# A hybrid decoder block in float32: operand addresses, eight projection pieces ahead of attention, and stores moved back

## The chip, the cores and the metric

The kernel runs on one core of a Trainium2 chip. It is judged by the device time of one launch in microseconds, over three runs; lower is better. TensorE (PE) multiplies, VectorE (DVE), ScalarE (ACT) and GpSimd (POOL) work element by element, and SyncE (SP) issues the transfers between the memories, one after the other in its queue.

## The reference, cut to what matters

One layer for one sequence of 2048 tokens of width 1024. Half of the input projection feeds eight heads of stick-breaking attention, the other half four groups of causal pooling over 2, 4, 8 and 16 tokens; both go through one output projection, and a SwiGLU FFN of width 2816 follows. Norms are modulated by a vector that is itself a product of c with w_cond.

```python
h = rmsnorm(x, g_mix_pre[l]) * (1.0 + scale_m) + shift_m
q, k, v, u = jnp.split(h @ w_in[l], [512, 1024, 1536], axis=-1)
attn = stick_breaking_attention(to_heads(q), to_heads(k), to_heads(v))
pool = pooling_mixer(u, w_pool[l], pool_scale[l])
mix = jnp.concatenate([attn, pool], axis=-1) @ w_out[l]
x = x + gate_m * rmsnorm(mix, g_mix_post[l])
h = rmsnorm(x, g_ffn_pre[l]) * (1.0 + scale_f) + shift_f
f = (jax.nn.silu(h @ w_gate[l]) * (h @ w_up[l])) @ w_down[l]
x = x + gate_f * rmsnorm(f, g_ffn_post[l])
```

Attention weighs a key by sigmoid(z) times the product of sigmoid(-z) over all later keys up to the query, with z = q.k / 8.

## The kernel before, in words

**Numbers.** A product of two float32 matrices is three matmuls of split operands: each operand is cut into a high part (a ScalarE copy to fp32r, L59) and the rest (a subtraction on VectorE or GpSimd, L60), and mm3 (L65) issues high x high, high x rest and rest x high. Each is 128x128 against 128x512.

**Order.** Inside manual_schedule (L140) TensorE, ScalarE, VectorE and GpSimd issue their instructions in the order in which the program writes them. SP is left out of that: a scheduler places its transfers, by readiness in its own model and, among those that are ready, by the place in the program. Once placed, SP takes them strictly one after the other: a store whose data isn't there holds every load behind it.

**Stages.** (1) Projections of token blocks 0 and 1 (a block is 512 tokens, a task is one 128-column chunk of q, k or u for one block). pieces (L434) yields after each of the eight mm3 of a task; run_small (L408) then does one small thing: an urgent one (taking a finished product out of its bank) or the next step of a pooling group. Beside it, rest_of_cond (L285) streams w_cond through four wc buffers and the four quarters of spare; VectorE sums it up (acc, L210). Weight chunks are loaded into w32 (two buffers, L424) 20 pieces ahead and split 14 to 5 pieces ahead (LOAD_AT, SPLIT_AT, L40). (2) v for all tokens (v_pieces, L480), with the tokens of blocks 2 and 3 prepared beside it. (3) Attention, 80 units of four steps (L984): z (L828), two sigmoids, a running product on VectorE (scan, L844 and L847), the product w on GpSimd (L852), four transposes (L863), a split, and the product with v (L878). Between its steps, fillers (L898) put the pieces that project q, k and u of blocks 2 and 3: N_PIECES = 217, spread in proportion to the area of the steps (goal, L1002). (4) The output projection. (5) The FFN in two halves of the tokens, gate and up then down, each a product of 2x2 blocks done with seven products instead of eight; a step of it is twelve matmuls. Its split weights come from operand (L1041): five of six from ring, every sixth from fx.

**What the change touches.** store_qk (L353) takes a finished q or k product, splits it into a buffer e (two of them for blocks 0 and 1) and stores it. pool_ops (L360) takes u, makes running sums on us0 and us1, then the mean um (L395, L399), and stores it (L400); um has one buffer, as up has bufs=1. take_chunk (L471) queues both. attending (L406) says that attention has begun.

**Places in memory.** Pools are stacked: const, c1, wst, up, att, qk from the left (later const, then ring and the FFN's token operands), and wsp, ha, hb, hc, tok, cond or wv from the right (later fx). Each tile's size is rounded up to 32 bytes for each partition. Before, const ends 288 bytes past a multiple of 512, so that ring and the FFN's operands behind it start there; up ends 192 past one, with vt and sg behind it; the six pr tiles of 513 words (2080 bytes each) lie between sg and w, so that w starts at 384, wth and wtl at 64, kt and qt at 128. On the right, all large tiles start at 480, but for xt in tok and the pools behind it (wvh and wvl among them), which start at 224.

Of the kernel before, what the change touches and what calls it, by code (L numbers as in the profile page):

```python
# [9 lines left out]
F32 = mybir.dt.float32  # L10
# [7 lines left out]
P = 128  # L18
# [10 lines left out]
TB = 512  # L29
# [4 lines left out]
OFF = 7  # L34
PRB = 6
# [9 lines left out]
def block_kernel(ctx, tc, x, c, w_cond, b_cond, g_mix_pre, g_mix_post, w_in, w_pool,  # L45
                 pool_scale, w_out, g_ffn_pre, g_ffn_post, w_gate, w_up, w_down, out):
    nc = tc.nc
# [6 lines left out]
    def raw(ap):  # L54
        return ap.bitcast(F32)

    def split(hi, lo, src, low=nc.vector):

        nc.scalar.copy(hi, src)  # L59
        low.tensor_tensor(lo, src, raw(hi), ALU.subtract)  # L60
# [12 lines left out]
    def open_pool(stack, name, bufs=1, side=None):  # L73
        kw = {"side": side} if side else {}
        return stack.enter_context(tc.tile_pool(name=name, bufs=bufs, reuse_waits="tile", **kw))

    dram = ctx.enter_context(tc.tile_pool(name="dram", bufs=1, space=DRAM))
    const = ctx.enter_context(tc.tile_pool(name="const", bufs=1))

    def dt(name, shape):  # L80
        return dram.tile(shape, F32, tag=name, name=name)
# [4 lines left out]
    mtd = [dt(f"mtd{i}", [KC, P, TB]) for i in range(NTB)]  # L86
# [16 lines left out]
    mods = {n: const.tile([P, KC], F32, tag=n, name=n) for n in ("af", "bf")}  # L103
    mods["am"], mods["bm"] = sumsq[:, 0:KC], sumsq[:, KC:]

    fx = None

    def ft(tag, name, shape=(P, TB)):
# [33 lines left out]
    c1 = open_pool(ph1, "c1")  # L142
# [26 lines left out]
        nc.gpsimd.memset(rcnt[:, j:j + 1], 1.0 / (j + 1))  # L169
    colv = c1.tile([P, 68], F32, tag="colv", name="colv")  # L170
    cs = c1.tile([P, KC], F32, tag="cs", name="cs")
    halo = [c1.tile([P, 16], F32, tag=f"halo{g}", name=f"halo{g}") for g in range(NG)]

    hts = ExitStack()
# [3 lines left out]
    pro = ExitStack()  # L178
    hc = open_pool(pro, "hc", side="right")
    tokp = open_pool(pro, "tok", bufs=2, side="right")  # L180
    condst = ExitStack()
    cond = open_pool(condst, "cond", bufs=2, side="right")
    ht = {}
# [169 lines left out]
    def store_qk(tb, ps, dst, name):  # L353
        pool, tag, bufs = (tokp, "e", 2) if tb < 2 else (wst, "e", 1)
        both = pool.tile([P, 2, TB], F32R, tag=tag, bufs=bufs, name=f"{name}_{tb}")
        split(both[:, 0], both[:, 1], ps)
        nc.sync.dma_start(dst[tb].rearrange("l p t -> p l t"), raw(both))
        stored.add((name[0], int(name[1]), tb))

    def pool_ops(tb, ps, g):  # L360

        win = 2 << g
        u = up.tile([P, 16 + TB], F32, tag="u", name=f"u{g}_{tb}")

        m = None
        if tb > 1:
            m = up.tile([P, TB], F32, tag="um", name=f"um{g}_{tb}")

        def take():
            if m is None:  # L370
                nc.scalar.copy(u[:, 16:], ps)
            else:
                nc.scalar.mul(u[:, 16:], ps, 1.0 / win)
                nc.scalar.copy(m, ps)
            if tb == 2:
                nc.scalar.mul(u[:, 0:16], halo[g], 1.0 / win)
            else:
                nc.gpsimd.tensor_copy(u[:, 0:16], halo[g])
            nc.gpsimd.tensor_copy(halo[g], u[:, TB:TB + 16])
        yield take  # L380
        prev, step, ahead, n = u, 1, 1, 0
        while step < win:
            cur = up.tile([P, 16 + TB], F32, tag=f"us{n % 2}", name=f"us{g}_{tb}_{step}")
            yield lambda: (nc.gpsimd if attending else nc.vector).tensor_tensor(cur[:, ahead:], prev[:, ahead:],
                                                  prev[:, ahead - step:16 + TB - step], ALU.add)
            prev, step, ahead, n = cur, 2 * step, ahead + 2 * step, n + 1
        if m is None:
            m = up.tile([P, TB], F32, tag="um", name=f"um{g}_{tb}")

        def mean():  # L390
            if tb > 1:
                nc.gpsimd.tensor_tensor(m, prev[:, 16:], m, ALU.subtract)
                nc.sync.dma_start(mtd[tb][4 + g], m)
                return
            nc.vector.scalar_tensor_tensor(m, prev[:, 16:], 1.0 / win, u[:, 16:], ALU.mult, ALU.subtract)  # L395
            if tb == 0:
                first = up.tile([P, 16], F32, tag="uf", name=f"uf{g}")
                nc.vector.tensor_tensor(first[:, 0:win], prev[:, 16:16 + win], rcnt[:, 0:win], ALU.mult)
                nc.vector.tensor_tensor(m[:, 0:win], first[:, 0:win], u[:, 16:16 + win], ALU.subtract)  # L399
            nc.sync.dma_start(mtd[tb][4 + g], m)  # L400
        yield mean


    small, urgent = [], []
    stored = set()
    attending = False  # L406

    def run_small():  # L408
        if urgent:
            urgent.pop(0)()  # L410
        elif small:
            op = next(small[0], None)
            if op is None:
                small.pop(0)
                run_small()
            else:
                op()
# [80 lines left out]
    def drain_small():  # L498
        while small or urgent:
            run_small()  # L500

    def weave(main, sides):

        done = [0] * len(sides)
        for n, _ in enumerate(main):
            for i, (ops, first, every) in enumerate(sides):
                if n >= first + done[i] * every:
                    done[i] += 1
                    next(ops, None)
        for ops, _, _ in sides:  # L510
            for _ in ops:
                pass
# [281 lines left out]


    att = open_pool(ph1, "att", bufs=2)
    qkp = open_pool(ph1, "qk", bufs=2)
    kv = {}

# [87 lines left out]
    def unit_loads(u):  # L887
        h, tb, sc = u
        if sc == tb:
            assert tb < 2 or {("q", h // 2, tb), ("k", h // 2, tb)} <= stored  # L890
            qts[h, tb] = block_loads(h, tb)
# [6 lines left out]
    def fillers():  # L898
        yield from pieces(1, chunks, tasks, [first_filler])
        while urgent:  # L900
            urgent.pop(0)()
# [3 lines left out]
    fill = fillers()  # L905
    N_PIECES = 9 * 2 * len(chunks) + 1
    units = [(h, tb, sc) for half in range(2) for h in range(HEADS) for tb in (2 * half, 2 * half + 1) for sc in range(tb, -1, -1)]
    area = [2.5 if tb == sc else 4.0 for _, tb, sc in units]
    wo, wo_next = [], 0
    HB_FREE = N_PIECES - 18  # L910
    END = 79
    POOL_EVERY = 2
    taken = 0
    attending = True
    begin = psum("z2", 1, "begin")
    nc.vector.memset(begin, 0.0)
# [4 lines left out]
    def wo_load():  # L921
        nonlocal wo_next
        for l in range(2):
            nc.sync.dma_start(raw(wo[wo_next][l]), wod[wo_next][l])
        wo_next += 1
# [24 lines left out]
    def mix_split(T, m32):  # L950
        mh = wsp.tile([P, KC, P], F32R, tag="wh", name=f"mh_{T}")
        ml = wsp.tile([P, KC, P], F32R, tag="wl", name=f"ml_{T}")
        for half in range(2):
            ks = slice(4 * half, 4 * half + 4)
            split(mh[:, ks], ml[:, ks], m32[:, ks])
        return T, mh, ml
# [26 lines left out]
    spent = 0.0  # L983
    for n in range(len(steps) + OFF):  # L984

        late_values = len(waiting) > LAG and waiting[0][0][1] == waiting[0][0][2] and waiting[0][1] == 0
        if len(waiting) > LAG and not late_values:
            values_step(*waiting.pop(0))
        if n < len(steps):
            u, i = steps[n]  # L990
            if i == 0:
                unit_loads(u)
            weights_step(u, i)
            spent += 2.5 if u[1] == u[2] else 4.0
        if len(scans) > 1 or n >= len(steps) and scans:
            scan_step(*scans.pop(0))
        if n >= OFF:
            u, b = steps[n - OFF]
            waiting.append((u, b, *turn_step(u, b)))
        if late_values:  # L1000
            values_step(*waiting.pop(0))
        goal = N_PIECES * spent / (4 * sum(area[:END]))  # L1002
        while fill is not None and taken < goal:
            taken += 1
            if next(fill, 0) == 0:
                fill = None

        if small and (n > len(steps) if fill is None and len(small) == 1 else n % POOL_EVERY == 0):
            run_small()
        for pool, here in ((hb, not wo and taken >= HB_FREE), (ha, len(wo) == 4 and fill is None)):  # L1010
            if here:
                hi, lo = (pool.tile([P, 4, D], F32R, tag=tag, name=f"wo_{pool.name}{tag}")
                          for tag in ("hi", "lo"))
                wo.extend((hi[:, k, :], lo[:, k, :]) for k in range(4))
        if wo_next < len(wo):
            wo_load()
        if n in FIRST_LOADS:
            firsts.append(mix_load(SEQUENCE[FIRST_LOADS.index(n)]))
        if n in FIRST_SPLITS:
            products.append(mix_products(*mix_split(*firsts.pop(0))))  # L1020
        if n in FIRST_ADDS:
            firsts[0] = mix_add(*firsts[0])
        if n >= len(steps):
            mix_pieces(PER_STEP)
# [690 lines left out]
```

## Time and profile before

| | us |
|---|---|
| median of 3 runs | 2284.33 (2283.15 to 2285.94) |
| the profiled execution | 2285.23 |
| its span | 2283.4 |

Stages in that execution: the projections to about 180 us, v to 286, attention from 292 to about 812, the output projection to about 1010, the FFN from there on. The page gives the engines' busy time, the clock that TensorE was granted, and the chain of work that ended last, followed back from the end. A row of the timeline holds start, duration, engine, line and operation, with its output and inputs, and in brackets the idle time ahead of it and who ended it. A matmul's duration includes its way through the array, so that one starts before the last has ended: the pace is the distance between starts. A row of the windows holds the stretch, its length, the busy time and count of TensorE, weight loads, VectorE, ScalarE and GpSimd, then the granted clock, the share of the DMA engines and GB/s. A row of the waits holds who waited for whom, the sum, the count and the longest.

### The profile page before, as it was taken

How to read it: one execution, taken by the hardware profiler on the slowest of the kernel's cores; microseconds unless marked ns; L12 is line 12 of the kernel's file. 1: busy time of each engine (PE TensorE's matmuls, PEld its weight loads, DVE VectorE, ACT ScalarE, POOL GpSimd, SP SyncE). 2: the span in 40 equal slices, each digit the busy share in tenths (PEclk: the TensorE clock that was granted, in tenths of full speed). 3: DMA queues.
4: the chain of work that ended last, by engine and by line, in shares of the span. 5: the costliest groups of instructions: out<-in, count | busy, mean ns of one | idle time of the engine just before them, and what ended most of it. 6: DMA issues, size and time to landing. Idle time of an engine off the chain costs nothing.

```text
span 2283.4 us, 33237 instructions
## 1 busy us (share of the span) xinstructions
PE 2247.0 (98%) x10605; PEld 1847.4 (81%) x10605; DVE 1619.5 (71%) x2212; ACT 1166.1 (51%) x2418; POOL 1295.7 (57%) x1607
## 2 busy tenths in 40 slices
PE   7999989999999999999999999999999999999998
PEld 5778878888888878887888888888888888888887
DVE  6774589999999966667656566786766565655566
ACT  4334579998899854443232323554533333334444
POOL 3552267787779965546777777331476565651003
PEclk9999999999999999999999999999999999999999
DMA  8885776634444356665545455776753332328654
GB/s 295 306 272 199 282 203 186 172 111 112 116 131 109 123 192 217 218 226 164 164 157 161 159 159 187 264 248 208 259 175 123 94 116 93 115 89 291 214 186 147
DMA packets 323979, 413.55 MB, mean 181 GB/s; under 512 B 20630, under 2 KB 189146, under 8 KB 323676
## 3 DMA queue, kind: packets, MB, share of 16 engines
q1 hardware_dynamic: 319484, 409.07, 55.7%
q10 hardware_dynamic: 4320, 2.36, 0.4%
q8 instruction: 83, 1.36, 0.2%
q14 instruction: 92, 0.75, 0.1%
HBM read 282.90 MB, written 128.45 MB: 180 GB/s over the span
## 4 chain that ended last, share of the span: by engine, by line
PE 90%; DVE 3%; ACT 2%; DMA 2%; POOL 2%; issue 1%; SPq 0%; DVEq 0%; POOLq 0%; ACTq 0%
PE wt L863 5%; PE t_g L69 3%; PE t_g L70 3%; PE t_u L70 3%; PE t_u L69 3%; PE t_u L71 3%; PE t_g L71 3%; PE dn0p L70 3%; PE dn0p L71 3%; PE dn0p L69 3%; PE dn1p L70 3%; PE dn1p L69 3%; PE dn1p L71 3%; PE b_u L70 3%; PE b_g L70 3%; PE b_g L69 3%
## 5 line engine op out<-in xcount | busy, mean ns | idle before, releaser
L852 POOL TENSOR_TENSOR w<-sg,pr 128x512 f32<-128x512 f32 (+2 forms) x320 | 306.7, 958 | 53.3 <-DVE pr L847 18.8
L1230 POOL TENSOR_TENSOR s<-s,cu 128x512 f32<-128x512 f32 x88 | 132.3, 1510 | 239.4 <-DVE cu L1229 146.5
L847 DVE TENSOR_TENSOR_SCAN pr<-pr,carry,begin 128x512 f32<-128x512 f32 x192 | 243.8, 1270 | 0.0
L831 ACT ACTIVATE sg<-z 128x512 f32<-128x512 f32 (+2 forms) x320 | 181.5, 567 | 54.4 <-PE z L829 44.3
L60 DVE TENSOR_TENSOR wtl<-wt,wth 128x512 fp32r<-128x512 f32 (+1 forms) x320 | 189.2, 591 | 19.9 <-ACT wth L59 18.2
L59 ACT CAST wth<-wt 128x512 fp32r<-128x512 f32 (+1 forms) x320 | 181.0, 567 | 11.9 <-PE wt L863 11.9
L833 ACT ACTIVATE pr<-z 128x512 f32<-128x512 f32 (+2 forms) x320 | 180.9, 565 | 0.0
L863 PE MATMUL wt<-ident,w 128*128 128x128 f32 x1088 | 172.2, 273 | 0.7 <-POOL pr L843 0.4
L60 DVE TENSOR_TENSOR u_s_l<-u_s,u_s_h 128x512 fp32r<-128x512 f32 x66 | 65.3, 989 | 145.9 <-ACT u_s_h L59 140.7
L863 PEld LDWEIGHTS wt<-ident,w 128*128 128x128 f32 x1088 | 134.0, 140 | 30.7 <-POOL pr L843 0.9
L1220 ACT ACTIVATE s<-s 128x512 f32<-128x512 f32 x88 | 55.7, 633 | 182.7 <-DVE s L1219 182.7
L878 PE MATMUL av<-wth,vt 128*128 128x512 f32 (+1 forms) x320 | 126.2, 394 | 1.7 <-ACT o L883 1.4
L828 PE MATMUL z<-kt,qt 128*128 128x512 f32 (+2 forms) x320 | 118.5, 370 | 6.6 <-DMA kt<-kd 5.1
L60 DVE TENSOR_TENSOR u_a_l<-u,u_a_h 128x512 fp32r<-128x512 f32 x66 | 73.0, 1108 | 71.0 <-ACT u_a_h L59 71.0
L70 PE MATMUL dn0p<-w0p_l,g0p_h 128*128 128x512 f32 x308 | 120.8, 392 | 0.6 <-DVE w0p_l L60 0.6
L69 PE MATMUL dn0p<-w0p_h,g0p_h 128*128 128x512 f32 x308 | 120.5, 391 | 0.0
L71 PE MATMUL dn0p<-w0p_h,g0p_l 128*128 128x512 f32 x308 | 120.3, 391 | 0.0
L879 PE MATMUL av<-wtl,vt 128*128 128x512 f32 (+1 forms) x320 | 117.6, 368 | 1.7 <-DVE wtl L60 1.4
L829 PE MATMUL z<-kt,qt 128*128 128x512 f32 (+2 forms) x320 | 117.1, 366 | 0.0
L844 DVE TENSOR_TENSOR_SCAN pr<-pr,zero,begin 128x128 f32<-128x128 f32 (+3 forms) x128 | 111.2, 870 | 7.0 <-ACT pr L833 6.6
L70 PE MATMUL dn1p<-w1p_l,g1p_h 128*128 128x512 f32 x292 | 114.4, 392 | 0.0
L69 PE MATMUL dn1p<-w1p_h,g1p_h 128*128 128x512 f32 x292 | 114.2, 391 | 0.0
(692 smaller groups left out, 7063.8 us busy)
## 6 DMA issues: line engine op xcount, KB each, us to landing
g<-in_w_gate_dram SPq DMA_DIRECT2D x42, 512.0 KB, 5.3
u<-in_w_up_dram SPq DMA_DIRECT2D x42, 512.0 KB, 4.1
wc<-in_w_cond_dram SPq DMA_DIRECT2D x32, 512.0 KB, 7.1
qt<-qd SPq DMA_DIRECT2D x64, 256.0 KB, 3.9
kt<-kd SPq DMA_DIRECT2D x96, 128.0 KB, 3.3
vt<-vd SPq DMA_DIRECT2D x48, 256.0 KB, 3.8
wd<-in_w_down_dram SPq DMA_DIRECT2D x44, 256.0 KB, 3.5
tdt<-wd SPq DMA_DIRECT2D x44, 256.0 KB, 2.0
```

The lines of the kernel that those rows point to most:

```text
L59: nc.scalar.copy(hi, src)
L60: low.tensor_tensor(lo, src, raw(hi), ALU.subtract)
L69: nc.tensor.matmul(ps, lh, rh, start=first and i == 0, stop=False)
L70: nc.tensor.matmul(ps, lh, rl, start=False, stop=False)
L71: nc.tensor.matmul(ps, ll, rh, start=False, stop=last and i == n - 1)
L831: nc.scalar.activation(sg[:, 0:L], z[:, 0:L], AF.Sigmoid, scale=0.125)
L833: nc.scalar.activation(pr[:, 0:L], z[:, 0:L], AF.Sigmoid, scale=-0.125)
L847: nc.vector.tensor_tensor_scan(keys, keys, begin, carry, ALU.mult, ALU.bypass)
L852: nc.gpsimd.tensor_tensor(w[:, 0:L], sg[:, 0:L], pr[:, 1:L + 1], ALU.mult)
L863: nc.tensor.transpose(wt[:, i * P:(i + 1) * P], wss[u][i][:, b * P:(b + 1) * P], ident)
L878: nc.tensor.matmul(av[:, lo0:], vb, wh[:, lo0:], start=first, stop=False)
L1230: nc.gpsimd.tensor_tensor(s, s, u, ALU.mult)
```

## The change

Three things. **Addresses:** lay_out allocates tiles that nothing uses. A pad of 192 bytes ends const, one of 96 bytes lies in c1, one of 64 bytes ends att, and one of 256 bytes lies in tok behind its small tiles, which now come first; in att the order is now vt, sg, w, wth, wtl, and pr and the carries behind them. With that, the large tiles of const's neighbours start 480 bytes past a multiple of 512 on both sides: ring and the FFN's operands, vt, sg, w, wth, wtl, kt, qt, wvh and wvl. The identity stays at 128, and the pr tiles keep their odd size. **Eight pieces:** the first eight pieces of the fillers (one task: q of head pair 0, block 2) are issued ahead of attention; the rest are spread over it as before. **Stores:** the store of a q or k product is issued four run_small later, that of a mean ten run_small later; run_stores counts them down, and drain_small or the start of attention issues what is left. In attention stores go at once, as before.

```diff
+    def lay_out(pool, tags, pad):
+        for tag, bufs, words in tags:
+            pool.tile([P, words], F32, tag=tag, bufs=bufs, name=f"first_{tag}")
+        pool.tile([P, pad], F32, tag="pad", bufs=1, name="pad")
+
+    lay_out(const, (), 48)
...
+    lay_out(c1, (), 24)
...
+    lay_out(tokp, (("ss", 2, 1), ("rs_v", 2, 1), ("rs_r", 4, 1)), 64)
...
-        nc.sync.dma_start(dst[tb].rearrange("l p t -> p l t"), raw(both))
+        later(4, lambda: nc.sync.dma_start(dst[tb].rearrange("l p t -> p l t"), raw(both)))
...
-            nc.sync.dma_start(mtd[tb][4 + g], m)
+            later(10, lambda: nc.sync.dma_start(mtd[tb][4 + g], m))
...
-    small, urgent = [], []
+    small, urgent, waiting_stores = [], [], []
+
+    def later(pieces, store):
+        if attending:
+            store()
+        else:
+            waiting_stores.append([pieces, store])
+
+    def run_stores(pieces):
+        for entry in list(waiting_stores):
+            entry[0] -= pieces
+            if entry[0] <= 0:
+                waiting_stores.remove(entry)
+                entry[1]()
...
     def run_small():
+        run_stores(1)
...
     def drain_small():
         while small or urgent:
             run_small()
+        run_stores(100)
...
+    lay_out(att, (("vt", 6, TB), ("sg", 5, TB), ("w", OFF + 4, TB), ("wth", 4, TB), ("wtl", 4, TB), ("pr", PRB, TB + 1),
+                  *((f"carry{i}", 2, 1) for i in range(4))), 16)
...
+    START = 8
     POOL_EVERY = 2
-    taken = 0
+    for _ in range(START):
+        next(fill)
+    taken = START
+    run_stores(100)
     attending = True
...
-        goal = N_PIECES * spent / (4 * sum(area[:END]))
+        goal = START + (N_PIECES - START) * spent / (4 * sum(area[:END]))
```

## The prediction

> **What bounds the kernel now.** I read the page first (busy shares, chain of waits), then TensorE's own waits, then the windows by stage.
>
> ```profile
> PE 2247.0 (98%) x10605; PEld 1847.4 (81%) x10605; DVE 1619.5 (71%) x2212; ACT 1166.1 (51%) x2418; POOL 1295.7 (57%) x1607
> ...
> PE 90%; DVE 3%; ACT 2%; DMA 2%; POOL 2%; issue 1%; SPq 0%; DVEq 0%; POOLq 0%; ACTq 0%
> ```
> ```profile
> PE z L828 <- DMA kt<-kd: 5.1, 1, 5.1
> PE u L71 <- POOL wu_l L60: 3.0, 1, 3.0
> ```
> TensorE works 98% of the span and 90% of the chain that ended last, so time comes only from two places: the few stalls of TensorE, and the pace of its matmuls. The two waits shown are the ones that this change can reach: the first z of attention waits for keys, and one projection waits for a split weight. Whether attention itself is TensorE's is less clear:
>
> ```profile
> 400.00:500.00 100.00, 100.00 (x579) 85.16 (x578) 97.79 (x132) 91.95 (x216) 80.06 (x177) 1.00 0.51 146
> 600.00:700.00 100.00, 100.00 (x565) 84.33 (x565) 98.39 (x123) 90.97 (x199) 77.82 (x171) 1.00 0.39 113
> ```
> Columns: TensorE, weight load, VectorE (97.8 and 98.4 of 100 us), ScalarE, GpSimd, clock, DMA. VectorE is 2% from being the bound there.
>
> **Part 1, addresses.** In the program of before, the pools on the left from ring on begin 288 bytes past a multiple of 512, and fx on the right 480 past one. const holds 672 bytes (the 128x128 identity 512, mhalf 32, sumsq 64, af and bf 32 each) from 128 on: 800 = 512 + 288. The new pad of 48 words (192 bytes) makes it 480, as on the right. In the FFN operand() takes every sixth operand from fx, so the two operands of a product differ by 0, 192 or 320 bytes modulo 512. Here are the first matmuls of six successive steps of 12:
>
> ```profile
> 1053.17 0.39 PE L69 MATMUL t_g<-t2h,g_s_h 128*128 128x512 f32 x1
> ...
> 1055.89 0.39 PE L69 MATMUL t_g<-t3h,g_s_h 128*128 128x512 f32 x1
> ...
> 1058.63 0.39 PE L69 MATMUL t_g<-t1h,g_s_h 128*128 128x512 f32 x1
> ...
> 1061.35 0.39 PE L69 MATMUL t_g<-t4h,g_a_h 128*128 128x512 f32 x1
> ...
> 1064.07 0.39 PE L69 MATMUL b_g<-b22h,g_s_h 128*128 128x512 f32 x1
> ...
> 1066.87 0.39 PE L69 MATMUL b_u<-b11h,u_a_h 128*128 128x512 f32 x1
> ```
> Twelve matmuls take 2.72 us where both operands lie in pools at 288 (t2, t1, t4), 2.74 with a weight from fx against tokens at 288 (t3, difference 192), and 2.80 with b22 on the right at 480 against a weight at 288 (difference 320). The size follows from the counts. Down: 2 x 7 phases x 11 chunks less the 4 held ones are 150 chunks, in each third the w operand lies in fx: 50 chunks at +0.08 us. Gate and up: 22 b22 steps in the first half, less those with a weight from fx, are 19 more at +0.08; about 48 steps at +0.025. Sum 69 x 0.08 + 48 x 0.025 = 5.5 + 1.2 = **6.7 us**, all on TensorE's path. I take -6.5 (bounds 0 and -7.5). In attention kt and qt already agree (both at 128), wth against vt differs by 128 and will agree; the trace has no case of it alone, so I count 0 (at most 1 us: 0.002 us for each of about 600 matmuls, the 192 case as the nearest). The pads themselves hold no instruction.
>
> The Trainium skill speaks against this part: SBUF — State Buffer, "Who interferes with whom", says that TensorE has two independent read ports and never waits on anyone. By that rule the part is worth 0. The rows above disagree with it by 0.08 us in 2.72, but they don't isolate the address from the pool it belongs to, so the rule's outcome is a rival below.
>
> **Part 2, stores later.** The chain of waits through the projections:
>
> ```profile
> 100.57 9.07 DMA wq<-in_w_in_dram
> ...
> 113.86 1.11 DVE um L395
> 115.27 0.33 SPq L400
> 115.65 0.42 SPq L202
> 116.12 5.94 DMA wu<-in_w_in_dram
> ...
> 125.46 2.55 POOL spare L264
> 128.00 1.68 POOL wu_l L60
> ```
> ```profile
> 108.62 1.22 DVE L275 TENSOR_TENSOR acc<-acc,spare 128x1024 f32<-128x1024 f32 x1
> ```
> ```profile
> 97.00 4.68 POOL L60 TENSOR_TENSOR wu_l<-wu,wu_h 128x256 fp32r<-128x256 f32 x4 [4.95 <-ACT wu_h L59]
> ```
> ```profile
> 129.73 0.50 PE L71 MATMUL u<-hth,wu_l 128*128 128x512 f32 x1 [2.96 <-POOL wu_l L60]
> ```
> SP stands before the store of um (L400) until VectorE has finished um, at 115.27; behind it are a load into spare (L202) and the load of wu, which ends in TensorE's wait of 2.96 us. The spare half is free at 109.84 (108.62 + 1.22), the earlier wu buffer at 101.7 (97.00 + 4.68). With the store ten pieces (10 x 3 x 0.227 = 6.8 us) further back, wu can be issued near 110.3 rather than 116.1. The DMA engines set a limit:
>
> ```profile
> 110.00:120.00 10.00, 9.74 (x50) 7.97 (x51) 8.06 (x10) 2.11 (x6) 6.55 (x8) 1.00 0.90 318
> 120.00:130.00 10.00, 7.04 (x31) 5.51 (x31) 6.49 (x8) 4.38 (x8) 6.04 (x5) 1.00 0.96 344
> ```
> They are 90 to 96% busy, so about 1.4 us of transfer time is to be had in these 20 us, and as much ahead of them; the reordering past the 0.25 MB store adds a little. And the stall has an aftermath:
>
> ```profile
> 126.00:130.00 4.00, 1.04 (x5) 0.58 (x4) 4.00 (x3) 0.47 (x1) 4.00 (x3) 1.00 1.01 333
> 130.00:134.00 4.00, 4.00 (x13) 3.16 (x13) 3.96 (x4) 0.43 (x2) 0.36 (x1) 0.66 0.98 317
> 292.00:296.00 4.00, 4.00 (x15) 3.35 (x15) 1.23 (x2) 1.40 (x5) 0.72 (x3) 0.61 1.08 240
> ```
> After both waits the granted clock is low: 13 matmuls in 4 us where 4 / 0.227 = 17.6 fit. 4.6 missing matmuls x 0.227 give 1.0 us in that window, and with the clock of the neighbours in proportion (a loss of 0.34 x 4 = 1.4 us of full clock) I count 1.5 us for each stall. The Trainium skill, TensorE: Matmul & The Clock Gate, "Part 1: The HAM clock gate", has the clock fall only after an idle window of about 3.4 us; by it a stall cut to half keeps the full clock, and half of the cure gives 1.5 + 1.5 = 3.0, where in proportion it would give 2.25. No run here shows such a stall yet.
>
> So removing the wait is worth 3.0 + 1.5 = 4.5; the other bound is 0. I take two thirds of it, **-3.0**, since the transfers give back 1.4 of the 3.0 us for certain and about as much more where wq's load (9.07 us) starts earlier; it is the least sure term. The risk: um has one buffer. The second block's mean comes eight pieces after the first's, its store ten, so VectorE, in order, may stand at the next mean until the store has landed; then the q and k splits, and acc with its wc buffers, are late behind it. The q and k stores move by four pieces and pass loads likewise; e has two buffers and q0, k0, q1 follow closely, but TensorE has no wait there: 0 (bounds -0.5, +1).
>
> **Part 3, eight pieces ahead of attention.** One task (q0, third token block): 24 matmuls x 0.227 = 5.45 us, moved in front of the first z.
>
> ```profile
> 284.21 0.62 SPq L811 DMA_DIRECT2D kt<-kd  x1
> 287.88 0.34 SPq L496 DMA_DIRECT2D vd<-ve  x1
> 288.26 0.46 SPq L811 DMA_DIRECT2D kt<-kd  x1
> ```
> ```profile
> 286.12 0.39 PE L71 MATMUL v<-wvh,htl 128*128 128x512 f32 x1
> 291.66 0.42 PE L828 MATMUL z<-kt,qt 128*128 128x128 f32 x1 [5.15 <-DMA kt<-kd]
> ```
> SP stands before the last store of v, the second half of the keys goes out at 288.26, and the first z starts at 291.66, 5.3 us later than a matmul behind 286.12 could. The eight pieces need nothing but weights split long before, and fill 286.35 to 291.8. z starts 0.15 us later than now; 5.45 us of TensorE's work is gone from attention, and the low clock from 292 on: at most 5.3 + 1.5 = 6.8. Taken back: the task before attention may use a bank of the z cycle (z1 by my count of the cycle), so the second z waits for q's copy and subtraction:
>
> ```profile
> 100.32 0.57 ACT L59 CAST k<-k 128x512 fp32r<-128x512 f32 x1
> 100.92 0.69 DVE L60 TENSOR_TENSOR k<-k,k 128x512 fp32r<-128x512 f32 x1
> ```
> 1.3 us after 291.8, against a z that would start near 292.4: 0.7. The ramp's latency through ScalarE and VectorE doesn't get shorter with the clock: 0.8. And VectorE:
>
> ```profile
> DVE wtl L60 <- ACT wth L59: 4.9, 16, 0.7
> ```
> In 400 to 700 it waits for the split alone, 4.9 us, so TensorE's saving of 5.45 in some 510 us (1.1%) just fits its 1.6 to 2.2% of idle time; 0.6 for where it doesn't. I take 6.8 - 2.1 = **-4.7** (bounds 0 and -6.8). If the cover is gone, VectorE sets attention's length and the part is worth nothing.
>
> **Sum.** -6.5 - 3.0 - 4.7 = -14.2. The profiled execution took 2285.23 us (its span 2283.4 and 1.8 around it), 0.9 above the median of the three runs, 2284.33; so 2271.0 on its scale and **2270** against the median.
>
> **Rivals.**
> 1. VectorE is the bound of attention. For it: 98.4% busy; against: TensorE, not VectorE, is without idle time. Part 3 falls away: 2270 + 4.7 = 2275.
> 2. The transfers, not the store, set wu's arrival (DMA 0.96): part 2 falls away, 2273; with rival 1 too, 2278.
> 3. The change doesn't do what its first words say: the pace belongs to something else of fx and the right side. Then 2270 + 6.5 = 2276.5. Against: three different paces for two pools, and b22 alone slow.
> 4. Slower: the single um buffer. If the next mean waits for its store to land, and the splits behind it hold a PSUM bank, TensorE stands at each of four groups.
>
> ```profile
> mtd<-um SPq DMA_DIRECT2D x3, 256.0 KB, 5.3
> ```
> Two pieces (1.4 us) and 5.3 us to landing are 6.7 us, a price of 4 x (6.7 + 1.5 of clock) = 33 if none is hidden; less parts 1 and 3, +22: 2306. It decides once the wait exceeds a task of eight pieces, 5.4 us, which is what another bank covers; if only the excess shows (1.3 each, without the clock) it is 5 us, and 2278. Against: VectorE makes the second um 5 us after the first, with sums between them, so much of the 6.7 is hidden.
>
> ```profile
> 120.22 0.69 DVE L395 SCALAR_TENSOR_TENSOR um<-us,u 128x512 f32<-128x512 f32 x1
> ```
>
> **How the numbers follow.** My forecast 0.56 (own range 2265 to 2275); rival 1 0.14, rival 2 0.08, both 0.08; rival 3 0.06; rival 4 0.08, of which 0.06 slower. The range 2263 to 2279 leaves out rival 4's upper end and double failures with losses. 0.2% (4.6 us) is about what a measurement of this kernel can tell from no change: faster needs under 2279.8, which all but rival 4 and about 0.05 of mixtures give: faster 0.88, same 0.06, slower 0.06.
>
> **What would show it.** Part 1: a step of 12 takes 2.72 us everywhere in the FFN, and 1050 to 2280 shrinks by 6 to 7 us; steps of 2.80 left over prove it wrong. Part 2: no wait of u on wu_l, no window near 130 with a clock of 0.66, a um store behind the wu load; a VectorE wait on the store proves rival 4. Part 3: no wait of z on kt over 1 us, full clock at 292, and attention (first z to the end of the last av) shorter by 4 to 6 us; if it is as long as before with new waits of av on wtl, rival 1 holds.

## The result and the profile after

| | before | after |
|---|---|---|
| median, 17 runs of each, us | 2285.53 (2282.52 to 2287.47) | 2279.49 (2278.38 to 2283.63) |
| profiled execution, us (its span) | 2285.23 (2283.4) | 2283.63 (2281.5) |

The ratio is 0.9978 (95% interval 0.9971 to 0.9985): faster by 0.22%, which is 5 us; the medians lie 6.0 us apart. 14 had been forecast. 2279.49 lies half a microsecond above the stated range. The profiled execution of the changed kernel is the longest of its 17; a second profile of it (the run a_after below) has a span of 2279.6, and shows the same waits at the same places.

First the page, TensorE's line and the chain of waits, then TensorE's own waits, of the changed kernel:

```profile
PE 2241.1 (98%) x10605; PEld 1849.6 (81%) x10605; DVE 1625.0 (71%) x2212; ACT 1164.2 (51%) x2418; POOL 1292.6 (57%) x1607
...
PE 89%; DVE 5%; ACT 2%; POOL 1%; issue 1%; DMA 1%; SPq 0%; DVEq 0%; POOLq 0%; ACTq 0%
```
```profile
PE u L69 <- DVE k L60: 6.3, 1, 6.3
...
PE z L855 <- DMA qt<-qd: 2.5, 1, 2.5
...
PE z L855 <- DMA kt<-kd: 2.3, 1, 2.3
...
PE z L855 <- DVE q L60: 1.2, 1, 1.2
```

TensorE is busy 5.9 us less for the same 10605 matmuls: that is pace. The two waits that were to go are gone: u no longer waits for wu_l, and the first z no longer for keys (the 2.3 at kt belong to a later z). But the four shown here stand in their place, and VectorE's share of the chain grew from 3% to 5%.

Where the time went, by stages cut at the same instructions. The last av lies at 836, among the first products of the output projection, later than the 812 given above for attention. The windows for the stage from the last matmul of v to the last av, and for the FFN from its first t_g to its last matmul (four earlier steps of it lie among the output projection); before:

```profile
286.12:836.00 549.88, 539.21 (x3027) 451.87 (x3026) 515.50 (x665) 474.77 (x1078) 427.95 (x920) 1.00 0.50 142
```
```profile
1016.63:2275.50 1258.87, 1256.44 (x5505) 1031.44 (x5503) 804.51 (x1056) 479.88 (x878) 657.67 (x460) 1.00 0.53 172
```
and after:

```profile
288.30:842.66 554.36, 544.06 (x3027) 454.14 (x3026) 515.04 (x665) 473.47 (x1078) 427.21 (x919) 0.99 0.50 140
```
```profile
1022.79:2273.40 1250.61, 1247.93 (x5505) 1031.78 (x5503) 809.57 (x1056) 478.98 (x878) 656.82 (x460) 1.00 0.53 173
```

| stage, us | before | after | second profile of after |
|---|---|---|---|
| start to the last matmul of v | 286.12 | 288.30 | 288.75 |
| that to the last av, the end of its first matmul (both kernels do the same work here) | 549.88 | 554.36 | 551.85 |
| output projection, to the first t_g of the FFN | 180.63 | 180.13 | 180.13 |
| FFN | 1258.87 | 1250.61 | 1250.70 |

The FFN gave 8.2 us, more than was forecast. The two earlier stages, where 3.0 and 4.7 us were to be saved, got 2.2 to 2.6 and 2.0 to 4.5 us longer. (The two profiles of the changed kernel differ by 2.5 us in the second of these; the kernel with 112 words, further down, shows where.)

**The new wait near 98.** Three rows of the chain of waits, two of VectorE's timeline and one of the windows, all of the changed kernel:

```profile
93.45 6.40 DMA mtd<-um
...
100.67 3.36 DVE acc L219
104.02 0.61 DVE k L60
```
```profile
94.77 1.21 DVE L60 TENSOR_TENSOR gs2xs<-acc,gs2xt 128x1024 fp32r<-128x1024 f32 x1
99.95 0.80 DVE L404 SCALAR_TENSOR_TENSOR um<-us,u 128x512 f32<-128x512 f32 x1 [3.96 <-DMA mtd<-um]
```
```profile
104.00:108.00 4.00, 3.32 (x8) 2.67 (x9) 4.00 (x7) 0.00 (x0) 0.00 (x0) 0.50 0.72 208
```

And SP's row of the same store before the change:

```profile
89.51 0.33 SPq L400 DMA_DIRECT2D mtd<-um  x1
```

VectorE is done with the split before at 95.98 (94.77 + 1.21) and wants to write the second block's mean into um. The first block's mean is still being stored: the store went out at 93.45, and its 6.40 us end at 99.85. So VectorE stands 3.96 us, then makes um, one step of acc that takes 3.36 us, and only then the split of k at 104.02, 6 us later than before, which the bank of the next u waits for: TensorE stands 6.3 us, and works at half clock (the windows row: 0.50) for the next four. VectorE stands at um a second time, 4.0 us up to 126.3, with no wait of TensorE behind it.

**The waits in attention.** SP's rows, TensorE's rows and one window of the changed kernel:

```profile
295.50 0.38 SPq L366 DMA_DIRECT2D qd<-q  x1
295.99 1.28 SPq L838 DMA_DIRECT2D kt<-kd  x2
```
```profile
295.53 0.39 PE L855 MATMUL z<-kt,qt 128*128 128x256 f32 x1 [1.23 <-DVE q L60]
...
299.86 0.30 PE L855 MATMUL z<-kt,qt 128*128 128x128 f32 x1 [2.30 <-DMA kt<-kd]
```
```profile
372.55 0.45 PE L855 MATMUL z<-kt,qt 128*128 128x128 f32 x1 [2.49 <-DMA qt<-qd]
```
```profile
300.00:304.00 4.00, 4.00 (x14) 3.43 (x15) 1.75 (x4) 2.25 (x7) 2.37 (x9) 0.57 1.08 234
```

The task that was put ahead leaves a q to be split and stored. SP stands in front of that store until the split is there, and the keys for the second unit go out behind it, at 295.99; the z that needs them stands 2.30 us, and the clock drops to 0.57 afterwards. The second z waits 1.23 us for the bank that this q occupied. Near 370 a third wait follows, for a qt; such a wait (1.2 to 3.1 us) is in every profile with eight pieces ahead and in none without them.

### The profile page after: what moved, and what is told of

The parts are those of the page before. It is cut to its first block, busy times and chain, and to the rows that moved or that the text cites. A ratio compares the mean times of both kernels' runs of the same rounds, so it can differ in the third digit from the quotient of the medians.

```text
span 2281.5 us, 33243 instructions
## 1 busy us (share of the span) xinstructions
PE 2241.1 (98%) x10605; PEld 1849.6 (81%) x10605; DVE 1625.0 (71%) x2212; ACT 1164.2 (51%) x2418; POOL 1292.6 (57%) x1607
## 4 chain that ended last, share of the span: by engine, by line
PE 89%; DVE 5%; ACT 2%; POOL 1%; issue 1%; DMA 1%; SPq 0%; DVEq 0%; POOLq 0%; ACTq 0%
PE wt L890 4%; PE t_g L69 3%; PE t_g L70 3%; PE t_u L70 3%; PE t_u L71 3%; PE t_u L69 3%; PE t_g L71 3%; PE dn0p L70 3%; PE dn0p L71 3%; PE dn0p L69 3%; PE dn1p L69 3%; PE dn1p L70 3%; PE dn1p L71 3%; PE b_g L70 3%; PE b_u L70 3%; PE b_u L71 3%
## 5 line engine op out<-in xcount | busy, mean ns | idle before, releaser
L59 ACT CAST g_s_h<-g_s 128x512 fp32r<-128x512 f32 x66 | 39.6, 621 | 152.6 <-POOL g_s L1193 80.6
L59 ACT CAST u_s_h<-u_s 128x512 fp32r<-128x512 f32 x66 | 38.6, 614 | 149.6 <-POOL u_s L1193 140.0
L71 PE MATMUL dn1p<-w1p_h,g1p_l 128*128 128x512 f32 x292 | 113.6, 389 | 0.0
```

The lines of the kernel that those rows point to most:

```text
L71: nc.tensor.matmul(ps, ll, rh, start=False, stop=last and i == n - 1)
```

## The experiments

### The three parts alone, and the changed kernel again

Each of three kernels keeps one part and takes the other two back. Addresses alone:

```diff
-        later(4, lambda: nc.sync.dma_start(dst[tb]..., raw(both)))
+        nc.sync.dma_start(dst[tb]..., raw(both))
-            later(10, lambda: nc.sync.dma_start(mtd[tb][4 + g], m))
+            nc.sync.dma_start(mtd[tb][4 + g], m)
-    START = 8
+    START = 0
```

> The addresses alone: the four pads, all stores at once, no piece ahead of attention. Theory A (the pace of a matmul hangs on the difference of its operands' addresses): the FFN, from the first t_g to the last matmul, gets 8.25 us shorter (4.16 at -3.33 to +2.09 and 2.83 before it in the full change's trace), nothing else moves by more than 1 us, the stalls of before (z on kt 5.1, u on wu_l 3.0) stay; 8 to 9 us below before. Rival (the FFN got shorter because something else of the change reached it, such as other transfer times): less than 3 us below before.

2275.53 us (2275.35 to 2277.76; before 2285.72), ratio 0.9963 (0.9949 to 0.9976): 10.2 us, nearly twice what the whole change gives. The FFN and TensorE's wait that part 2 was to remove:

```profile
1014.92:2265.60 1250.68, 1247.95 (x5505) 1031.79 (x5503) 807.19 (x1056) 478.96 (x878) 657.73 (x460) 1.00 0.54 173
```
```profile
PE u L71 <- POOL wu_l L60: 2.8, 1, 2.8
```
```profile
130.00:134.00 4.00, 4.00 (x19) 3.31 (x18) 3.77 (x4) 1.50 (x5) 1.02 (x1) 1.00 1.01 325
```

The FFN's 8.2 us are all there. The wait for wu_l stays, but in this execution no low clock followed it: 1.00 where before had 0.66, 19 matmuls in place of 13, an estimate of 6 x 0.227 = 1.4 us. That may be part of the 2.0 us that the FFN doesn't account for. They lie within what one execution differs from the next: this kernel's stage up to the last matmul of v ends at 283.15, and that of the kernel with the eight pieces alone, whose program is that of before up to there, at 284.44, both earlier than the 286.12 of before. In the stage behind it, up to the last av, the addresses gave nothing: 551.64 us, before 549.88.

Stores alone (the four pads out, START = 0):

> The later stores alone, no pads, no piece ahead. Theory S (the store of um, 10 pieces late, keeps the single um buffer while VectorE stands before the next mean, 8 pieces on): no wait of u on wu_l, but TensorE stands some 6 us near 98 for the split of k, with a low clock behind it; up to the last v 2 to 3 us longer than before, and the whole 2 to 3 us above before. Rival (the wait near 98 was an accident of the one profiled execution, the store doing what was forecast): no wait over 1 us near 98, 3 to 4.5 us below before.

2289.34 us (11 runs), ratio 1.0018 (1.0009 to 1.0026): 3.6 us slower, near an estimate from the waits alone (6.3 and 2 us of half clock lost, 3.0 and 1.5 won). The same wait as in the changed kernel, from VectorE's timeline and TensorE's waits:

```profile
100.40 0.76 DVE L401 SCALAR_TENSOR_TENSOR um<-us,u 128x512 f32<-128x512 f32 x1 [3.84 <-DMA mtd<-um]
```
```profile
PE u L69 <- DVE k L60: 6.1, 1, 6.1
```

Eight pieces alone (the four pads out, both stores at once):

> Eight pieces ahead alone, no pads, all stores at once. Theory H (what the eight pieces cover is given back in attention by the next late transfers: the wait for kt before the third column of z, a wait for qt near 370, and the low clock behind both): first z near 292, attention to the last av not shorter than before, the whole between 1 us below and 3 us above before. Rival (the wait for qt was an accident of one execution; the cover is worth what was forecast, less the z waits of 1.2 and 2.3 us): 2 to 4 us below before.

2284.37 us (11 runs), ratio 0.9996 (0.9987 to 1.0005): 1.3 us, not clear of nothing. The waits for the q split (1.1), kt (2.4) and qt (1.2) are there.

> The changed kernel as it is, a second profile of it. If the waits of its first profile belong to the kernel, u on k (6.3 us), z on kt (2.3) and z on qt (2.5) are there again at the same places; if the first profile, the longest of 17 executions, held accidents, one or more of them is missing and the span is some 4 us shorter. Time 5 to 7 us below before.

2280.29 us (11 runs), ratio 0.9982 (0.9973 to 0.9990); all three waits again (u on k 6.3, z on kt 2.3, z on qt 2.9). They belong to the kernel. The parts alone add up to -10.2 + 3.6 - 1.3 = -7.9, measured together -5.4.

### Is it the addresses?

The next two kernels are the changed one with another number in one line, so that only the place of what follows const on the left moves against the right side.

```diff
-    lay_out(const, (), 48)
+    lay_out(const, (), 112)
```

> The changed kernel with 112 words of padding in place of 48 behind the constants: the left side's operands go to 224, the right side's stay at 480, so that every product that was at a difference of 192 or 320 before now is at 256; all other products stay equal. Nothing else differs. If the address sets the pace: the FFN's steps with one operand from the right side take other than 2.72 us again (2.74 to 2.85), and the FFN gets 3 to 10 us longer than in the changed kernel. If the pace belongs to the pools or to something else of the change: 2.72 everywhere, the time within 1 us of the changed kernel.

> The same with 32 words: the left side at 416, the right at 480, differences 64 and 448. If the address sets the pace: 2.72 us for steps whose two operands lie on the left, another value for those with one operand on the right, and its size says whether a small difference costs less than 192 or 320 did (0.02 and 0.08 a step). If it is the pools: 2.72 everywhere and the time within 1 us of the changed kernel.

The FFN of the kernel with 112 words (difference 256), then of that with 32 words (64 and 448), in windows:

```profile
1022.60:2273.92 1251.32, 1248.49 (x5505) 1031.76 (x5503) 806.54 (x1056) 478.60 (x878) 657.84 (x460) 1.00 0.53 173
```
```profile
1023.60:2285.25 1261.65, 1259.20 (x5505) 1032.19 (x5503) 813.31 (x1056) 479.88 (x878) 656.43 (x460) 1.00 0.53 172
```

and the starts of two steps each, and of the steps behind them: t3 (a weight from the right) and b22 (tokens from the right). With 112 words:

```profile
1061.61 0.39 PE L69 MATMUL t_g<-t3h,g_s_h 128*128 128x512 f32 x1
...
1064.33 0.39 PE L69 MATMUL t_g<-t1h,g_s_h 128*128 128x512 f32 x1
...
1069.77 0.39 PE L69 MATMUL b_g<-b22h,g_s_h 128*128 128x512 f32 x1
...
1072.49 0.39 PE L69 MATMUL b_u<-b11h,u_a_h 128*128 128x512 f32 x1
```
With 32 words:

```profile
1062.87 0.40 PE L69 MATMUL t_g<-t3h,g_s_h 128*128 128x512 f32 x1
...
1065.67 0.39 PE L69 MATMUL t_g<-t1h,g_s_h 128*128 128x512 f32 x1
...
1071.14 0.40 PE L69 MATMUL b_g<-b22h,g_s_h 128*128 128x512 f32 x1
...
1073.90 0.40 PE L69 MATMUL b_u<-b11h,u_a_h 128*128 128x512 f32 x1
```

In the changed kernel the b22 step and the one behind it:

```profile
1069.91 0.39 PE L69 MATMUL b_g<-b22h,g_s_h 128*128 128x512 f32 x1
...
1072.63 0.39 PE L69 MATMUL b_u<-b11h,u_a_h 128*128 128x512 f32 x1
...
1075.35 0.39 PE L69 MATMUL b_u<-b21h,u_a_h 128*128 128x512 f32 x1
```

Address of the weight less that of the tokens, modulo 512, and twelve matmuls:

| kernel | t3 step | b22 step | FFN, us |
|---|---|---|---|
| before | 192: 2.74 | 320: 2.80 | 1258.87 |
| changed | 0: 2.72 | 0: 2.72 | 1250.61 |
| 112 words | 256: 2.72 | 256: 2.72 | 1251.32 |
| 32 words | 64: 2.80 | 448: 2.76 | 1261.65 |

One constant moves the FFN by 11 us, so it is the address and no property of the pools. A difference of 256 costs nothing in the pace; as far as these values show it, what counts is the difference modulo 256: 64 (and 320) costs 0.08 us a step, 192 (and 448) 0.02 to 0.04. And the step behind such a step is slow too, though its own operands agree: with 32 words the two steps from 1065.67 to 1071.14 take 5.47 us, with 112 words 5.44. The expectation for 112 words was wrong in that: 256 was expected to cost. The medians: 2291.17 us (ratio 1.0026, 1.0017 to 1.0036) with 32 words, 10.9 above the changed kernel; 2283.01 with 112 (0.9991, 0.9982 to 1.0000), whose ten runs lie in two groups, 2280.1 to 2281.9 and 2284.1 to 2285.6. The FFN accounts for 0.7 us of that. Its profiled execution (2284.18) is of the second group, and its stage from v to the last av takes 554.38 us, as in the first profile of the changed kernel (2283.63) and 2.5 more than in the second (2281.69). The window behind the wait for qt, with 112 words and then in that second profile:

```profile
372.00:382.00 10.00, 9.64 (x43) 8.61 (x44) 4.47 (x8) 5.58 (x13) 3.57 (x11) 0.66 0.32 80
372.00:382.00 10.00, 8.52 (x52) 7.39 (x53) 6.94 (x10) 7.18 (x17) 3.73 (x13) 1.00 0.37 100
```

The first profile of the changed kernel has 0.66 there as well. So a low clock behind the wait for qt comes in some executions and not in others; that every run of the second group has it is not shown.

### Is it um's one buffer?

The mean of block 0 goes to a tile that lies unused at that time, so that block 1's has um for itself. Addresses and later stores stay, no piece ahead:

```diff
-            m = up.tile([P, TB], F32, tag="um", ...)
+            m = up.tile([P, TB], F32, tag="um", ...) if tb else wst.tile([P, 2, TB], F32, tag="e", bufs=1, ...)[:, 0]
-    START = 8
+    START = 0
```

> Addresses and later stores with a second buffer for um (the means of the first token block go to another, unused tile, so that the mean of the second block has its own), no piece ahead. Theory S (the single um buffer makes VectorE wait near 96 to 100): no wait of um on the store, no wait of u on k (6.3 us before), and, the forecast of the stores' move being otherwise right, none of u on wu_l either: 3 to 4.5 us below the addresses alone (2275.5), 2271 to 2272.5. Rival (SP's changed order or the transfers, not the buffer, make VectorE late): u on k keeps 3 us or more, 2277 to 2280.

2272.85 us (five runs), ratio 0.9951 (0.9938 to 0.9963). VectorE's timeline at the same place, and all of TensorE's waits between 85 and 140:

```profile
96.08 0.68 DVE L404 SCALAR_TENSOR_TENSOR um<-us,u 128x512 f32<-128x512 f32 x1
96.69 1.27 DVE L219 SCALAR_TENSOR_TENSOR acc<-wc,cs,acc 128x1024 f32<-128x1024 f32 x1
98.07 0.69 DVE L60 TENSOR_TENSOR k<-k,k 128x512 fp32r<-128x512 f32 x1
```
```profile
PE gp L249 <- DVE gs2xs L60: 0.7, 1, 0.7
PE u L69 <- DVE k L60: 0.3, 1, 0.3
```

um follows at once, k is split 6 us earlier than in the changed kernel, and the wait for wu_l is gone too. So the later stores do what they were forecast to do, once um has a second place: 2.7 us below the addresses alone by the medians, 1.8 when each is taken against the kernel before as it was measured beside it (forecast 3.0).

The stores of q and k alone, four pieces later, um at once:

> Addresses and the stores of q and k four pieces later, the store of um at once, no piece ahead. Theory S (um alone makes the new wait): no wait of u on k, the wait of u on wu_l stays near 3 us, within 1 us of the addresses alone, 2274.5 to 2276.5. Rival (the e buffers of q and k have a part in it): u on k shows 1 us or more, 2277 to 2279.

2276.76 us (2275.01 to 2278.56), ratio 0.9963 (0.9950 to 0.9975). The wait on k is down to 0.2 us, so e has no part in it; the time is slightly above what was expected. Its wait for wu_l, and the clock behind it:

```profile
127.30 0.50 PE L71 MATMUL u<-hth,wu_l 128*128 128x512 f32 x1 [1.97 <-POOL wu_l L60]
```
```profile
126.00:130.00 4.00, 2.71 (x8) 2.19 (x9) 4.00 (x4) 0.00 (x0) 1.93 (x2) 0.76 1.07 360
130.00:134.00 4.00, 4.00 (x15) 3.18 (x15) 2.63 (x3) 2.18 (x6) 2.37 (x3) 0.81 1.03 404
```

### What eats the eight pieces

> Addresses and eight pieces ahead, all stores at once. If the parts add: 2275.5 - 1.3 = 2274.2, between 2273.5 and 2275.5, with z waiting for the q split (1.2), for kt (2.3) and for qt near 365 (1.2 to 2.9). Rival (the later stores and the eight pieces get in each other's way, which is why the full change has less than its sum): 2272.5 or less.

2276.76 us (2274.09 to 2279.44): the parts do not add, there is nothing below the addresses alone. The stage from v to the last av takes 551.92 us, with the addresses alone 551.64. Then, with the q and k stores late as well, the store of the q computed ahead is put behind the key loads:

```diff
-    run_stores(100)
     attending = True
...
+        if n == 8:
+            run_stores(100)
```

> Addresses, q and k stores four pieces later, um at once, eight pieces ahead, but the store of the q that is computed ahead goes out at step 8 of attention instead of in front of it. Theory Q (SP stands before that store until the split of q is done, 293.4 to 295.5 in the first profile, and the keys of the third column, which z then waits 2.3 us for, are queued behind it): that wait falls under 1 us, with less low clock behind it, attention 2 to 3 us shorter, 1 to 3.5 us below addresses and pieces alone. Rival (the keys come late because of the buffer they wait for or of the transfers): the wait for kt stays above 1.8 us, no difference above 0.7 us.

2276.51 us (2274.01 to 2277.32): no difference in the median, though the wait for kt fell from 2.5 to 0.7 us and the stage to 547.90. This execution reached the last matmul of v 1.9 us later than the one without the moved store (286.96 to 285.05). The later stores of q and k lie ahead of that, but the kernel with these alone, whose program is the same up to there, reached it at 283.63: one profile of this stage says little. Both were therefore tried on the kernel with two places for um, where the stage is entered without the other stalls, and twice. The changed kernel whole, with the second place for um:

> The changed kernel whole, with a second buffer for um and nothing else. If the waits at um's buffer are all that the later stores cost: 7 to 9 us of the changed kernel's 98 to 125 us stretch come back, 2272 to 2274, with neither u on k nor u on wu_l, and eight pieces ahead worth 0 to 1 us against the same without them (2272.85). If other waits follow behind: 2275 or more.

2271.80 us (five runs, 0.9944, 0.9932 to 0.9957). With the moved store too:

> The changed kernel with a second buffer for um and with the store of the q that is computed ahead put at step 8 of attention. If both cures add: no wait over 1 us of u on k, u on wu_l and z on kt, the wait of z for qt near 365 (2 us) left, 1 to 3 us below the one without the moved store, 2269.5 to 2272. If what the moved store gains is lost in attention to VectorE: within 0.7 us of it.

2272.49 us (2268.23 to 2272.76; 0.9941, 0.9928 to 0.9953). The four measured beside each other, the last with the q computed ahead in the bank mm:

```diff
-            ps = mm_ps(f"{kind}{m}_{tb}", attending)
+            ps = mm_ps(f"{kind}{m}_{tb}", th == 1)
```

> Addresses, later stores, second um buffer, no piece ahead, again, as the ground that the next three stand on: 2272 to 2273.5, the wait of z on kt 5.1 us.

> The same with eight pieces ahead, again. Theory W (the part gives back 2.4 us at kt, 1.2 at the q split and 2 to 3 at qt with low clock behind): 0 to 1.5 us below the one without. Rival (its worth was hidden by scatter): 3 us or more below.

> The same with the ahead task's q store at step 8 of attention, again. Theory W: z on kt under 1 us, attention (last v to last av) 4 us shorter than without pieces ahead, 2 to 4 us below the one without pieces and 1.5 to 3 below the one with the store in front. Rival (VectorE bounds attention, so that a removed wait of TensorE comes back as waits for wtl): within 1 us of the one without pieces, waits of av on wtl 1 us or more longer.

> The same, and the q computed ahead uses the bank mm instead of a bank of the z cycle, so that the second z doesn't wait for q's split. Theory W: the wait of z on the q split (1.2 us) is gone and about 1 us of it shows in the time. Rival (the ramp through ScalarE and VectorE, or the keys, end that stretch anyway): the second z waits for something else that ends within 0.3 us of it, no difference.

| two places for um, and | median, first / second time | of both, ten runs | stage from v to the last av |
|---|---|---|---|
| no piece ahead | 2272.85 / 2272.99 | 2272.98 | 551.25, 551.40 |
| eight pieces | 2271.80 / 2273.67 | 2272.53 | 550.42, 552.45 |
| eight pieces, store moved | 2272.49 / 2270.58 | 2271.34 | 546.99, 547.19 |
| that, and q in mm | - / 2272.93 | | 549.95 |

The stage in windows, of no piece ahead and of the moved store (the first time of each), and SP's rows of the latter:

```profile
280.51:831.76 551.25, 539.98 (x3027) 451.57 (x3026) 515.89 (x665) 474.93 (x1078) 427.78 (x919) 1.00 0.51 142
```
```profile
281.31:828.30 546.99, 539.46 (x3027) 450.08 (x3026) 514.89 (x665) 472.90 (x1078) 427.26 (x919) 1.00 0.51 142
```
```profile
286.18 1.19 SPq L838 DMA_DIRECT2D kt<-kd  x2
...
288.51 0.36 SPq L366 DMA_DIRECT2D qd<-q  x1
```

The keys now go ahead of the store (z waits 0.5 and 1.4 us for kt, the second above the 1 us expected, and 2.5 and 2.3 with the store in front), and in both profiles the stage is 4.2 us shorter than without pieces ahead, though VectorE is as busy as ever: the forecast for the part was 4.7. With the store in front the stage is about as long as without the part. So the stage shows what the part lost, and VectorE is not the bound that gives it back. The median shows only 1.6 of the 4.2 us: the two profiles with the moved store reach the last matmul of v 0.8 to 2.8 us later than those without pieces, and one of them loses 0.6 to 1.2 us between attention and FFN. Why, and whether it is more than scatter, stays open.

The other bank did not help: the median is 2.35 us above that with the moved store alone (the five runs of each overlap), and the stage 2.8 us longer. Two of TensorE's rows of that kernel:

```profile
281.79 0.50 PE L69 MATMUL q<-hth,wq_h 128*128 128x512 f32 x1 [1.40 <-DVE ve L60]
...
291.59 0.30 PE L855 MATMUL z<-kt,qt 128*128 128x128 f32 x1 [1.24 <-ACT pr L860]
```

z no longer waits for q's split, but the q computed ahead now waits 1.40 us for the bank mm, which the split of v holds, and a later z waits for ScalarE instead.

## Why the prediction was wrong

**What bounds the kernel** held: what could be traced of the time won and lost came from stalls of TensorE, the clock behind them, and the pace of its matmuls.

**Part 1, forecast -6.5, bound -7.5; measured -8.2.** Right in mechanism, mis-sized. Of the 8.2, the matmuls at 320 gave 5.5 (as worked out), those at 192 1.5 (1.2 forecast), and 1.4 came from matmuls whose own operands agreed already: over 4112 of them the mean distance between starts fell by 0.36 ns. The forecast gave those nothing, and this is the term that was too small. (The wait of dn0p for w0p_l, 0.6 before and 0.9 after, takes 0.3 back.) They are not spread evenly: most of the 1.4 lies in the steps right behind one at 320. The prediction's last row, of b11 behind b22, starts at 1066.87; the next two steps of before start here:

```profile
1069.61 0.39 PE L69 MATMUL b_u<-b21h,u_a_h 128*128 128x512 f32 x1
...
1072.33 0.39 PE L69 MATMUL t_u<-t2h,u_s_h 128*128 128x512 f32 x1
```

b11 takes 2.74 us, b21 behind it 2.72; 64 such steps (14 of b11, 50 of down) at 0.02 are an estimate of 1.3. Rival 3 falls: with 32 words of padding in place of 48, and nothing else changed, the FFN takes 1261.65 us in place of 1250.61. With it falls the 0 that the prediction drew from the Trainium skill's rule (SBUF — State Buffer, "Who interferes with whom", that TensorE never waits on anyone).

**Part 2, forecast -3.0; alone +3.6.** The step that failed: "VectorE makes the second um 5 us after the first, with sums between them, so much of the 6.7 is hidden", and with it the 0.08 for rival 4. Of the 6.7 some was hidden from VectorE: the store went out 3.94 us later than before (93.45 and 89.51), took 6.40 us, and VectorE stood 3.96. But the step of acc behind it took 3.36 us in place of 1.27, so that the split of k came 6 us late, and of this nothing was hidden from TensorE, neither by the sums nor by another bank: it stood 6.3. So the price of one place was about right (6.7 + 1.5 of clock forecast, 6.3 and some 2 us of half clock measured), though in part by luck, since a third of it came from acc; it was paid at one place instead of four. The forecast gain itself was about right: with a second place for um the wait u on wu_l is gone and u on k is 0.3, for 1.8 to 2.7 us. So the sum's term had a condition that was named as a risk, priced, and given too little weight.

**Part 3, forecast -4.7; alone -1.3, with the rest +1.2 to -1.1.** The first z starts 5.67 us after the last matmul of v, 5.54 before: 0.13 later, forecast 0.15; and the wait for the bank of the z cycle came (1.23 us for 0.7 forecast). The step that failed is "no wait of z on kt over 1 us, full clock": the q task was counted in matmuls, not with its store, which stands in SP's queue ahead of the next keys; the 2.1 taken back in the sum has no term for it. That brought 2.3 us at kt and the low clock back. The wait of 2.5 near 370 came with the part too, but what makes that qt late was not isolated. With the store out of the way the stage gives 4.2 us in two profiles. Rival 1 (VectorE) does not hold. How much of the 4.2 reaches the median (1.6 over ten runs of each) stays open.

**The range** ended at 2279 because rival 4 was held apart with 0.06 above it. Parts 2 and 3 both failing was rival 1 + 2 at 2278; one of them turning into a loss lay outside.

## What to carry to other kernels

A store that is issued later keeps its buffer longer: before moving it, compare its new landing time (here 6.4 us) with the next write of the buffer on its in-order engine, and add a buffer first. Work that is moved into a gap brings its own entries to every queue; a load behind a store that waits for a product is late by that product. And where operand addresses differ, measure the pace of the products by pairs of pools: a few bytes of padding were worth more here than both reorderings.

## What the runs showed of the hardware

TensorE's pace depends on the difference of its two operands' addresses, modulo 256 as far as six values show it: 2.72 us for twelve 512-column products at 0 and 256, 2.74 to 2.76 at 192 and 448, 2.80 at 64 and 320. The effect reaches into the products behind: 2.74 for twelve whose operands agree, right after twelve at 320.

The clock is lowered after some short stalls and not after some longer ones: 0.76 and 0.81 after a wait of 1.97 us with the q and k stores late, 1.00 after 2.79 us with the addresses alone; and in two profiles of the changed kernel 0.66 after 2.49 us, 1.00 after 2.95. So half a stall need not save the clock, as the prediction had it from the Trainium skill (TensorE: Matmul & The Clock Gate, "Part 1: The HAM clock gate", a drop only after an idle window of about 3.4 us): that rule gives no drop in any of these cases. An estimate of what this alone moves a time by, from one execution to the next, is 1.4 us (19 and 13 matmuls near 130) to 2.5 us (the stage of attention in the two profiles of the changed kernel).

One step of acc took 3.36 us in the changed kernel, in both of its profiles and with the stores alone (1.27 in the same place with two places for um), while GpSimd added its spare, in GpSimd's timeline:

```profile
100.52 2.42 POOL L273 TENSOR_TENSOR spare<-spare 128x1024 f32<-128x1024 f32 x1 [0.32 <-ACT spare L270]
```

Whether the one slowed the other was not tried.
